# Other urgencies for the mixers' steps in a two-layer hybrid trunk: one list of ranks and six of its offsets

## The chip, the cores and the metric

The kernel runs on one core of one Trainium2 chip. Times are device microseconds (us) of that core. TensorE does the matrix products, VectorE and ScalarE the elementwise work and the moves out of PSUM, GpSimd small tables, and SyncE issues nearly all DMAs. Where the profile says PE, PEld, DVE, ACT, POOL and SP it means TensorE's products, TensorE's weight loads, VectorE, ScalarE, GpSimd and SyncE.

## The reference

Two layers over 256 positions of 1024 channels. Each layer normalises its input, makes one wide projection, runs three mixers on parts of it, gates and sums their outputs, projects, and ends in a squared-ReLU MLP:

```python
def hybrid_layer(x, pos, ...):
    h = rms_norm(x, g_mix)
    z = h @ w_in
    c_q, c_kv, k_rope, u2, q_nsa, kv_nsa, gate_nsa, gate_mix = jnp.split(z, SPLIT_IDX, axis=-1)
    o_a = mla_mixer(c_q, c_kv, k_rope, ...)          # latent attention, 8 heads
    o_b = conv_mixer(u2, ...)                        # gated 31-tap causal convolution
    o_c = nsa_mixer(q_nsa, kv_nsa, gate_nsa, ...)    # attention over compressed, selected and windowed keys
    g_a, g_b, g_c = jnp.split(jax.nn.sigmoid(gate_mix...), N_MIXERS, axis=-1)
    x = x + (g_a * o_a + g_b * o_b + g_c * o_c) @ w_out
    h = rms_norm(x, g_ffn)
    x = x + jnp.square(jax.nn.relu(h @ w_ff1)) @ w_ff2
    return x
```

In both attentions a block of 128 queries makes scores, a softmax over them, and then the **value products**, probabilities times values:

```python
s = jnp.einsum('bqhd,bkhd->bhqk', qb, k) * scale
p = masked_softmax(s, mask)
o = jnp.einsum('bhqk,bkhd->bqhd', p, v)              # 64 value channels a head
```

## The kernel before, in words

**Precision.** The large products split both operands into a high and a low part in a fast single-pass 32-bit format and sum three products (`gemm_a`, L176, and `gemm_b`, L168). The weights arrive as 512 KB pieces by SyncE; ScalarE makes the high part (L162) and VectorE the low one (L163). The attention's value products, the transposes and a few others stay in plain float32, where one product of the program is two TensorE instructions.

**A layer's stages.** First the norm and the projections whose output has positions on partitions (`psA`). Then the mixers with the rest of the wide projection (`psB`, 24 instructions a 128-column tile) and the output projections of each mixer (`wo`). Then the product with `w_out`, then the MLP (`ff`, `f`).

**Steps and urgencies.** The mixers' stage is cut into 58 steps, traced in the order of the list `TRACE`. A step is for instance ("qk", 1), the norm, rotation and transposes of one half's queries and keys; ("gt", m, i), two 128-column tiles of mixer m's gates with their two weight pieces; ("nsa", j) and ("mla", j), half the heads of an attention; ("mq", b) and ("mk", b), the latent attention's queries and keys of one half of the positions; ("tap", i), three or four of the convolution's taps on VectorE; ("cn",), the convolution's norm; ("wo", m, c), a quarter of mixer m's output projection; ("csc",), the scores against the compressed keys; ("lr", n) and ("lrn",), the low-rank inputs and their norms. Each step gets the number 1000 times its place in the list `URGENCY`, and each instruction of the step carries that number:

```python
for name, *args in TRACE:
    tc.cur_priority = base + 1000 * PRIO[(name, *args)]
    steps[name](*args)
```

A planner then writes out the order of each engine's instructions when the program is built: of those that its own cost table takes to be ready, and whose buffer is free, the one with the smallest number goes first. On the chip that order is fixed, and an engine waits at its next instruction until that one can run.

**Late parts.** Some steps raise or lower the number inside, by the table `OFF`: the transposes of `qk` by `qk0` and `qk1` (L433), the compression by `ckv` and `cmp` (L470, L482), the end of `csc` (L549), the transposes of the probabilities by `nT` and `mT` (L583), the heads' transposes by `hT` (L704), and the value products by `nO` (L613) and `mO` (L641).

**The value products.** `nsa_attention` (L594) has three blocks for each j: both pairs of heads for the first 128 queries, then each pair for the last 128. A block makes scores (`nS`, L606), two softmax units (L562), whose probabilities are transposed (`nT`, L586) and copied to SBUF by ScalarE (`nPT`, L588), and the value products `nO` (L621):

```python
for g in range(2):
    gs = slice(64 * g, 64 * g + 64)
    c = j * T + b * P
    mm(po[gs, c:c + P], lhsT=vsw[:, kb, z, gs], rhs=PTs[g][:, u * P:(u + 1) * P], ...)
```

A value product has 64 weight columns and writes 64 of PSUM's partitions, so TensorE's array is tiled by 64 columns for it, and by 128 for its neighbours; the two products of g = 0 and g = 1 lie in the two halves of the array. There are 24 of them for each j, which is 48 TensorE instructions. They end with two products with the compressed keys' probabilities (L625, 128 columns), after which `po`, a PSUM bank of which there is one, is split into `oh` and `ol` and free for the next. `mla_attention` (L629) does the same with three blocks of 8 instructions for each j (`mO`, L649). The compression has products of 32 weight columns (`cmp`, L486 and L498) and one of 32 rows (L512). The probabilities and their transposes live in the tile `pa`, of which there are 6.

Of the kernel before, what the change touches and what calls it, by code (L numbers as in the profile page):

```python
# [53 lines left out]
for _n, _w in _CST:  # L54
# [20 lines left out]
URGENCY = [("csc",), ("mq", 1), ("a1",), ("a",), ("qk", 1), ("lr", 0), ("lr", 1), ("qk", 0), ("mq", 0), ("mk", 0),  # L75
           ("ckv",), ("a2",), ("gt", 1, 2), ("mk", 1), ("glu", 3), ("a0",), ("lr", 2), ("tap", 2), ("gt", 2, 2),
           ("glu", 0), ("glu", 1), ("mla", 1), ("glu", 2), ("mla", 0), ("nsa", 1), ("gt", 2, 0), ("tap", 0),
# [4 lines left out]
PRIO = {s: i for i, s in enumerate(URGENCY)}  # L82

OFF = {"qk0": 11500, "qk1": 6000, "ckv": -10500, "cmp": 14500, "csc": 14500, "nT": 5000, "mT": 12500,
       "nO": 19000, "mO": -8000, "hT": -5500}


@with_exitstack
def trunk_kernel(ctx: ExitStack, tc: tile.TileContext, A, out, depth=DEPTH):
# [8 lines left out]
    def psum(tag, name):  # L98
        return pp.tile([P, 512], F32, tag=tag, name=name, bufs={"mm": 2, "at": 2, "pt": 2, "po": 1, "ch": 1}[tag])
# [149 lines left out]
    def rope(X, n, half, ct, st, name, eng=None):  # L249

        eng = eng or nc.vector
        p = X.shape[0]
        r = 2 * half
        a = sp.tile([P, n, r], F32, tag="ra%d" % (n * r), name=name + "_ra", bufs=2 if n * r > 64 else 1)[:p]
        c = sp.tile([P, n, r], F32, tag="rb%d" % (n * r), name=name + "_rb", bufs=2 if n * r > 64 else 1)[:p]
        ctb = bc(ct.rearrange("p (o r) -> p o r", o=1), [p, n, r])
        stb = bc(st.rearrange("p (o r) -> p o r", o=1), [p, n, r])
        eng.tensor_tensor(out=a, in0=X[:, :, 0:r], in1=ctb, op=ALU.mult)
        eng.tensor_tensor(out=c[:, :, 0:half], in0=X[:, :, half:r], in1=stb[:, :, 0:half], op=ALU.mult)
        eng.tensor_tensor(out=c[:, :, half:r], in0=X[:, :, 0:half], in1=stb[:, :, half:r], op=ALU.mult)  # L260
        eng.tensor_tensor(out=X[:, :, 0:r], in0=a, in1=c, op=ALU.add)

    def layer(l):
# [162 lines left out]
        def nsa_qk(b):  # L426
# [5 lines left out]
            rope(kd.rearrange("p j o d -> p (j o) d"), 8, RN // 2, tk_n[0][:, b], tk_n[1][:, b], "rkn")  # L432
            tc.cur_priority += OFF[("qk0", "qk1")[b]]  # L433
            bs = slice(b * P, (b + 1) * P)
# [23 lines left out]
        def compress_kv():  # L458
            KD = ap_.tile([P, 4, T], F32, tag="big", name="KD", bufs=BIG)
            for b in range(NB):  # L460
# [7 lines left out]
                else:  # L468
                    act(KD[64:128, :, b * P - 1:(b + 1) * P - 1], ptv[64:128], AF.Copy)
            tc.cur_priority += OFF["ckv"]  # L470
            for xi, (wn, pe, w2) in enumerate((("ck1", "pek", "ck2"), ("cv1", "pev", "cv2"))):
# [8 lines left out]
                for i in range(2):  # L480
                    nc.sync.dma_start(out=w1[:, 8 * i:8 * i + 8].rearrange("p k n -> p (k n)"), in_=A[wn][l, i])
                tc.cur_priority += OFF["cmp"]  # L482

# [41 lines left out]
        def compress_scores():  # L525
# [22 lines left out]
            sgv = sg.rearrange("p b (g j n) -> p b j g n", g=2, n=3)  # L548
            tc.cur_priority += OFF["csc"]  # L549
            for b in range(NB):  # L550
# [11 lines left out]
        def softmax_unit(pS, n, gate, name):  # L562
# [19 lines left out]
            now = tc.cur_priority  # L582
            tc.cur_priority += OFF[name + "T"]  # L583
            pt = psum("pt", name + "T")
# [9 lines left out]
        def nsa_attention(jp, o):  # L594
# [3 lines left out]
            for b, js in ((0, (0, 1)), (1, (0,)), (1, (1,))):  # L598
# [13 lines left out]
                now = tc.cur_priority  # L612
                tc.cur_priority += OFF["nO"]  # L613
                for i, j in enumerate(js):
# [483 lines left out]
```

## Time and profile before

| what | value |
|---|---|
| median of 3 runs | 914.36 us (911.64 to 2772.54) |
| the profiled execution | 915.6 us, of which the span from first to last instruction is 913.8 us |
| TensorE busy | 891.2 us, 98% of the span |
| VectorE, ScalarE busy | 654.0 us, 540.4 us |
| mean granted TensorE clock | 0.996 |

A busy share is taken over the whole span. A layer is some 450 us long; its mixers' stage is the first half of it, the MLP the second. TensorE's instructions overlap, so the time that one really takes of the engine is read from start to start, not from its duration.

### The profile page before, as it was taken

Reading aid. Unit: us, or ns where it says so; the run is one execution under the profiler, and the core shown is the slowest. Engines: PE = TensorE matmul, PEld = TensorE weight load, DVE = VectorE, ACT = ScalarE, POOL = GpSimd, SP = SyncE. Lnnn points to the kernel's source line nnn. Section 1 sums busy time; section 2 is a strip of 40 time slices with the busy share of each in tenths; the row PEclk is TensorE's granted clock in tenths of the full one; section 3 lists DMA queues with packets and bytes.
Section 4 is the critical chain, followed back from the end, with each engine's and each line's share of the span. In section 5 each row is a group of like instructions: output and inputs, shape, how many; then the busy total and the mean of one; then the engine's idle time right before and its main releaser. Section 6 shows DMA issues by size and latency. Waiting matters only on the chain.

```text
span 913.8 us, 16151 instructions
## 1 busy us (share of the span) xinstructions
PE 891.2 (98%) x6222; PEld 799.5 (87%) x6222; DVE 654.0 (72%) x1451; ACT 540.4 (59%) x1001; POOL 27.6 (3%) x81
## 2 busy tenths in 40 slices
PE   5999999999999999999999899999999999999998
PEld 4889998689988999999988898977899899999996
DVE  6499899975786755555586998998659685555552
ACT  5467576798456645444354656769967374554430
POOL 4110010000001000000000000000000000000000
PEclk9999999999999999999999999999999999999999
DMA  9335632453664865554452446134446466666501
GB/s 356 141 105 201 231 105 64 141 184 118 205 207 132 310 188 185 190 195 157 138 176 100 138 134 239 59 133 162 142 159 221 129 247 234 188 192 194 188 1 47
DMA packets 42749, 151.55 MB, mean 166 GB/s; under 512 B 4784, under 2 KB 5200, under 8 KB 42672
## 3 DMA queue, kind: packets, MB, share of 16 engines
q1 hardware_dynamic: 42480, 149.99, 49.2%
q8 instruction: 49, 0.80, 0.4%
q0 software_dynamic: 192, 0.53, 0.2%
q14 instruction: 28, 0.23, 0.1%
HBM read 149.45 MB, written 1.05 MB: 165 GB/s over the span
## 4 chain that ended last, share of the span: by engine, by line
PE 90%; DVE 6%; ACT 2%; issue 1%; DMA 1%; SPq 0%; DVEq 0%; ACTq 0%
PE ff L173 7%; PE ff L174 7%; PE ff L172 7%; PE f L180 6%; PE f L181 6%; PE f L182 6%; PE psB L172 6%; PE psB L174 6%; PE psB L173 6%; PE wo L172 3%; PE wo L173 3%; PE wo L174 2%; PE psA L182 2%; PE psA L180 2%; PE psA L181 2%; PE uq L669 2%
## 5 line engine op out<-in xcount | busy, mean ns | idle before, releaser
L163 DVE TENSOR_TENSOR lo<-raw,hi 128x1024 fp32r<-128x1024 f32 (+1 forms) x266 | 316.8, 1210 | 159.9 <-ACT hi L162 120.4
L162 ACT ACTIVATE hi<-raw 128x1024 fp32r<-128x1024 f32 (+1 forms) x266 | 271.8, 1047 | 224.5 <-PE ff L173 74.1
L172 PE MATMUL psB<-hh,hi 128*128 128x256 f32 x592 | 170.0, 288 | 2.6 <-ACT ug L780 2.5
L174 PE MATMUL psB<-hh,lo 128*128 128x256 f32 x592 | 171.0, 290 | 0.7 <-DVE lo L163 0.6
L173 PE MATMUL psB<-hl,hi 128*128 128x256 f32 x592 | 168.4, 285 | 0.0
L173 PE MATMUL ff<-l,hi 128*128 128x256 f32 x512 | 144.2, 282 | 0.0
L172 PE MATMUL ff<-h,hi 128*128 128x256 f32 x512 | 143.9, 281 | 0.0
L174 PE MATMUL ff<-h,lo 128*128 128x256 f32 x512 | 143.6, 281 | 0.0
L172 PEld LDWEIGHTS psB<-hh,hi 128*128 128x128 f32 x592 | 112.8, 191 | 6.3 <-ACT ug L780 3.0
L174 PEld LDWEIGHTS psB<-hh,lo 128*128 128x128 f32 x592 | 112.6, 191 | 3.2 <-DVE lo L163 1.5
L173 PEld LDWEIGHTS psB<-hl,hi 128*128 128x128 f32 x592 | 112.5, 190 | 1.1 <-issue 0.7
L789 DVE SCALAR_TENSOR_TENSOR ca<-upad,cols,ca 128x256 f32<-128x256 f32 x240 | 102.3, 476 | 0.2
L180 PE MATMUL f<-hi,rh 128*128 128x512 f32 x256 | 100.3, 392 | 0.0
L181 PE MATMUL f<-lo,rh 128*128 128x512 f32 x256 | 100.1, 391 | 0.0
L182 PE MATMUL f<-hi,rl 128*128 128x512 f32 x256 | 100.0, 390 | 0.0
L173 PEld LDWEIGHTS ff<-l,hi 128*128 128x128 f32 x512 | 98.0, 191 | 1.8 <-DVE l L217 0.8
L172 PEld LDWEIGHTS ff<-h,hi 128*128 128x128 f32 x512 | 96.1, 188 | 1.3
L174 PEld LDWEIGHTS ff<-h,lo 128*128 128x128 f32 x512 | 96.1, 188 | 0.0
L182 PEld LDWEIGHTS f<-hi,rl 128*128 128x128 f32 x256 | 48.1, 188 | 10.9 <-DVE rl L929 0.7
L180 PEld LDWEIGHTS f<-hi,rh 128*128 128x128 f32 x256 | 48.1, 188 | 9.2
L181 PEld LDWEIGHTS f<-lo,rh 128*128 128x128 f32 x256 | 48.2, 188 | 9.1
L180 PE MATMUL psA<-hi,hh 128*128 128x512 f32 (+1 forms) x96 | 36.4, 380 | 1.5 <-ACT hh L185 1.5
(283 smaller groups left out, 1438.7 us busy)
## 6 DMA issues: line engine op xcount, KB each, us to landing
raw<-in_ff_dram SPq DMA_DIRECT2D x128, 512.0 KB, 4.3
raw<-in_wB_dram SPq DMA_DIRECT2D x74, 512.0 KB, 4.2
raw<-in_wA_dram SPq DMA_DIRECT2D x16, 512.0 KB, 6.5
raw<-in_w_out_dram SPq DMA_DIRECT2D x16, 512.0 KB, 4.2
raw<-in_wo_nsa_dram SPq DMA_DIRECT2D x8, 512.0 KB, 4.3
raw<-in_wo_mla_dram SPq DMA_DIRECT2D x8, 512.0 KB, 4.2
raw<-in_wconv_dram SPq DMA_DIRECT2D x8, 512.0 KB, 3.6
raw<-in_wA_dram SPq DMA_DIRECT2D x8, 312.0 KB, 5.2
```

The source lines that it names most:

```text
L162: act(hi, r, AF.Copy)
L163: tt(out=lo, in0=r, in1=hi.bitcast(F32), op=ALU.subtract)
L172: mm(ps, lhsT=wh(kw), rhs=ah(ka), start=(first and i == 0), stop=False)
L173: mm(ps, lhsT=wh(kw), rhs=al(ka), start=False, stop=False)
L174: mm(ps, lhsT=wl(kw), rhs=ah(ka), start=False, stop=(last and i == n - 1))
L180: mm(ps, lhsT=ah(ka), rhs=wh(kw), start=(first and i == 0), stop=False)
L181: mm(ps, lhsT=ah(ka), rhs=wl(kw), start=False, stop=False)
L182: mm(ps, lhsT=al(ka), rhs=wh(kw), start=False, stop=(last and i == n - 1))
L669: mm(ps[:, :n], lhsT=cq[:, k, b * P:(b + 1) * P], rhs=w[i][:, c0:c0 + n], start=(i == 0), stop=(i == len(ks) - 1))
L789: stt(out=ca[:, i], in0=upad[:, i, k:k + T], scalar=K("wdw", 31 * i + k), in1=ca[:, i], op0=ALU.mult, op1=ALU.add)
```

## The change

The list `URGENCY` is put in another order and six entries of `OFF` get other values. No instruction, tile or buffer is added or taken away; `TRACE` stays. The changed order brings TensorE's array from one tiling to another 64 times in the whole program, where it was 92 times.

```diff
-URGENCY = [("csc",), ("mq", 1), ("a1",), ("a",), ("qk", 1), ("lr", 0), ("lr", 1), ("qk", 0), ("mq", 0), ("mk", 0),
-           ("ckv",), ("a2",), ("gt", 1, 2), ("mk", 1), ("glu", 3), ("a0",), ("lr", 2), ("tap", 2), ("gt", 2, 2),
-           ("glu", 0), ("glu", 1), ("mla", 1), ("glu", 2), ("mla", 0), ("nsa", 1), ("gt", 2, 0), ("tap", 0),
-           ("nsa", 0), ("tap", 1), ("gt", 2, 1), ("lrn",), ("gt", 0, 0), ("wo", 0, 0), ("gt", 2, 3), ("gt", 1, 0),
-           ("wo", 2, 0), ("tap", 7), ("tap", 4), ("gt", 0, 3), ("gt", 0, 1), ("tap", 6), ("tap", 3), ("cn",),
-           ("wo", 0, 1), ("gt", 1, 1), ("gt", 0, 2), ("wo", 0, 2), ("gt", 1, 3), ("wo", 2, 1), ("tap", 5),
-           ("wo", 0, 3), ("wo", 2, 2), ("wo", 2, 3), ("wo", 1, 0), ("wo", 1, 1), ("wo", 1, 2), ("rk",), ("wo", 1, 3)]
+URGENCY = [("mq", 1), ("a",), ("csc",), ("qk", 1), ("gt", 1, 3), ("a1",), ("lr", 0), ("lr", 1), ("qk", 0), ("mq", 0),
+           ("a0",), ("ckv",), ("a2",), ("glu", 3), ("gt", 1, 2), ("tap", 2), ("lr", 2), ("mk", 1), ("glu", 0),
+           ("mla", 0), ("glu", 1), ("mla", 1), ("mk", 0), ("glu", 2), ("gt", 2, 2), ("nsa", 1), ("gt", 2, 0),
+           ("tap", 0), ("nsa", 0), ("wo", 0, 0), ("tap", 1), ("gt", 2, 1), ("lrn",), ("gt", 0, 0), ("tap", 7),
+           ("gt", 2, 3), ("gt", 1, 0), ("gt", 0, 3), ("wo", 2, 0), ("gt", 1, 1), ("gt", 0, 1), ("tap", 4), ("cn",),
+           ("tap", 6), ("tap", 3), ("wo", 2, 1), ("wo", 0, 1), ("wo", 2, 2), ("gt", 0, 2), ("wo", 0, 2), ("tap", 5),
+           ("wo", 0, 3), ("wo", 2, 3), ("wo", 1, 0), ("wo", 1, 1), ("wo", 1, 2), ("rk",), ("wo", 1, 3)]
...
-OFF = {"qk0": 11500, "qk1": 6000, "ckv": -10500, "cmp": 14500, "csc": 14500, "nT": 5000, "mT": 12500,
-       "nO": 19000, "mO": -8000, "hT": -5500}
+OFF = {"qk0": 11500, "qk1": 11000, "ckv": -10500, "cmp": 15000, "csc": 6000, "nT": 4000, "mT": 14500,
+       "nO": 19000, "mO": -6000, "hT": -5500}
```

## Rows read from the trace of the kernel before

**Rows 1.** The page's busy times: us, share of the span, instructions.

```profile
PE 891.2 (98%) x6222; PEld 799.5 (87%) x6222; DVE 654.0 (72%) x1451; ACT 540.4 (59%) x1001; POOL 27.6 (3%) x81
```

**Rows 2.** Busy time by stretch, mixers' stage of layer 1: stretch, its length, engines, clock, DMA.

```profile
46.20:75.40 29.20, 26.22 (x217) 24.90 (x215) 27.90 (x65) 18.66 (x30) 2.70 (x10) 1.00 0.44 142
106.50:140.80 34.30, 34.07 (x320) 31.48 (x318) 32.83 (x121) 25.21 (x66) 2.29 (x2) 1.00 0.39 138
140.80:171.00 30.20, 30.05 (x216) 23.58 (x215) 28.93 (x105) 20.71 (x63) 0.00 (x0) 1.00 0.35 113
171.00:199.30 28.30, 28.21 (x175) 21.22 (x176) 24.96 (x115) 25.02 (x56) 1.05 (x4) 1.00 0.52 174
199.30:227.00 27.70, 27.69 (x243) 25.70 (x241) 15.58 (x41) 25.70 (x63) 0.20 (x1) 1.00 0.35 114
```

**Rows 3.** TensorE in order of time, 172.6 to 175.5 us: start, time, what.

```profile
174.52 0.28 PE L172 MATMUL psB<-hh,hi 128*128 128x256 f32 x1
174.64 0.28 PE L173 MATMUL psB<-hl,hi 128*128 128x256 f32 x1
174.84 0.43 PE L621 MATMUL nO<-nPT,vsw 128*64 128x128 f32 x2
175.21 0.39 PE L174 MATMUL psB<-hh,lo 128*128 128x256 f32 x1
175.43 0.28 PE L172 MATMUL psB<-hh,hi 128*128 128x256 f32 x1
```

**Rows 4.** TensorE in order of time, 207.9 to 209.7 us.

```profile
208.36 0.28 PE L172 MATMUL psB<-hh,hi 128*128 128x256 f32 x1
208.57 0.66 PE L649 MATMUL mO<-mPT,Vm 128*64 128x128 f32 x8
209.16 0.92 PE L638 MATMUL mS<-kTm,qTm 96*128 96x256 f32 x3
```

**Rows 5.** TensorE in order of time, 140.4 to 147.3 us.

```profile
140.83 1.52 PE L621 MATMUL nO<-nPT,vsw 128*64 128x128 f32 x22
...
142.71 0.44 PE L621 MATMUL nO<-nPT,vsw 128*64 128x128 f32 x4
143.08 0.66 PE L586 MATMUL nT<-cst,nP 128*128 128x128 f32 x4
143.67 1.85 PE L621 MATMUL nO<-nPT,vsw 128*64 128x128 f32 x22
```

**Rows 6.** Busy time of L621 alone in stretches around its groups, second j of layer 1.

```profile
156.90:157.90 1.00, 0.87 (x10) 0.63 (x10) 1.00 0.00 0
160.30:161.00 0.70, 0.65 (x6) 0.41 (x6) 1.00 0.00 0
169.80:171.00 1.20, 1.09 (x14) 0.85 (x14) 1.00 0.89 273
...
197.90:198.40 0.50, 0.43 (x2) 0.19 (x2) 1.00 0.76 311
```

**Rows 7.** The program's value products of the first attention by line: count, busy us, mean ns, idle.

```profile
L621 PE MATMUL nO<-nPT,vsw 128*64 128x128 f32 x192 | 17.9, 285 | 0.2
```

**Rows 8.** Who TensorE waited for in 46 to 76 us: us, times, longest.

```profile
PE psB L172 <- ACT ug L780: 1.3, 1, 1.3
PE qS_p L438 <- DVE qn L261: 1.0, 1, 1.0
```

**Rows 9.** TensorE in order of time, 95.6 to 102.2 us.

```profile
96.04 2.29 PE L680 MATMUL css<-ones,csq 128*128 128x1 f32 x20
```

**Rows 10.** Busy time by stretch, columns as in group 2.

```profile
98.30:101.70 3.40, 3.40 (x19) 3.40 (x18) 3.17 (x9) 0.00 (x0) 0.00 (x0) 0.50 0.86 283
...
140.40:143.80 3.40, 3.40 (x39) 2.62 (x39) 3.40 (x13) 2.44 (x7) 0.00 (x0) 1.00 0.00 0
143.80:147.20 3.40, 3.30 (x31) 2.69 (x31) 3.40 (x11) 2.22 (x10) 0.00 (x0) 1.00 0.03 5
```

**Rows 11.** The page's DMA issues: count, KB each, us to landing.

```profile
raw<-in_wB_dram SPq DMA_DIRECT2D x74, 512.0 KB, 4.2
```

## The prediction, made before the change was run

> **What bounds the kernel now.** I read the busy times first. TensorE works 891 of 913.8 us [rows 1], so the kernel ends when TensorE's queue ends, and a change of order helps only as far as it takes time out of that queue: less work in it, or fewer waits. The next view is busy time by stretch, for the mixers' stage, the only one whose order changes. From 106 us on TensorE has no idle time worth a name (0.23 us in 34.3, 0.15 in 30.2, 0.09 in 28.3, 0.01 in 27.7), and only from 46 to 75 us it waits, 3.0 us in 29.2 [rows 2]. VectorE is almost as full there: 27.9 of 29.2, 32.8 of 34.3 and 28.9 of 30.2 us, and has room only later, 3.3 us in 171 to 199 and 12.1 us in 199 to 227 [rows 2]. The third view is TensorE in order of time around the groups of 64-column products, since a busy engine hides the cost of changing its tiling: it must be read from start to start.
>
> **What a change of tiling costs.** A product of the wide projection starts 0.12 us after the one before it (174.52 to 174.64). The first value product behind one starts after 0.20 us (174.64 to 174.84) [rows 3], or 0.21 (208.36 to 208.57) [rows 4]: 0.08 to 0.09 us more. Inside a group, 4 instructions take 0.37 us to the start of the next group (142.71 to 143.08) [rows 5], and 8 take 0.59 (208.57 to 209.16) [rows 4]. So four more cost 0.22, or 0.055 each; 8 would cost 0.44, and the other 0.15 us is the group's own loss, at its start and its end. The first product behind the group keeps its successor back as well: 0.22 us (175.21 to 175.43) instead of 0.12 [rows 3], 0.10 more. Together 0.09 + 0.15 + 0.10 = 0.34 us for a group, which is two changes: 0.17 us each.
>
> By the Trainium skill this could be cheaper. "TensorEngine Tiling (Array Packing)", section Key Properties, says that a new tiling mode drains the engine, and "TensorE: Matmul & The Clock Gate", section "Step-by-step: what each phase is for", puts the array's draining at some 128 cycles: an estimate of 0.053 us at 2.4 GHz, and 28 x 0.053 = 1.5 us in all. The trace disagrees, with 0.17 us a change; I go by the trace.
>
> **What the change removes.** From 92 to 64 is 28 changes, 14 groups, 7 in each layer. The first j's value products already stand in three groups, of 22, 4 and 22 instructions [rows 5]. The second j's 48 are scattered from 156.9 to 198.4 us in nine groups, of 10, 6, 14, 2, 2, 4, 4, 4 and 2 (the first three and the last are in [rows 6]); layer 2 has as many again (192 in all) [rows 7]. Seven groups fewer a layer is just what is left over when these nine become two, so that is where I place them. 14 x 0.34 = **4.8 us** less work in TensorE's queue, all of it where that queue has no idle time.
>
> A second, smaller term: a group of 2 instructions takes 0.37 us (174.84 to 175.21) [rows 3], as long as one of 4. A lone product leaves the other half of the array empty, and costs 0.11 us that a pair would share. The groups of 10, 6, 14, 2, 2 and 2 are of odd numbers of products, so six stand alone in a layer. If they meet their partners, three times 0.11 us go in each layer: **0.7 us**. Bounds for both terms: no partner met, and only the inside and the exit paid (0.25 us a group), 3.5 us; every group as dear as the lone ones (0.08 + 0.26 + 0.10 = 0.44), 6.2 us. I take 4.8 + 0.7 = 5.5.
>
> **What the change moves, and what I cost at nothing.** ("gt", 1, 3) goes from place 47 to 4, but writes a tile that ("gt", 1, 0) allocates, at 36: it comes right behind that and no earlier. Two 512 KB loads and their splits on ScalarE and VectorE come forward with it in SyncE's queue; such a load lands 4.2 us after its issue [rows 11], and the DMA engines are 0.33 to 0.55 busy in this stage [rows 2], so they have room. The other gates, ("wo", 2, 1) and ("wo", 2, 2) change places by a few, each with its loads; the number of bytes and of splits is the same. Cover for all of this is the queue of ready gates and output projections, which filled TensorE to 27.69 of 27.70 us even while the second attention ran [rows 2]; if it fails, TensorE waits by the microsecond, which is the slower rival below. The taps go back a few places ("tap", 4, 6 and 3, from 37, 40 and 41 to 41, 43 and 44), which frees VectorE earlier and puts the convolution's norm later; its output projections are last in the list anyway, and VectorE has 12.1 us free from 199 to 227 us. ("mk", 0) goes from 9 to 22, behind ("mk", 1), and the two halves of the second attention change places: their first scores may come some microseconds later, with the same cover. GpSimd has 27.6 us of work in all and its steps keep their places [rows 1].
>
> **The early waits.** The late part of ("qk", 1) goes from number 10000 to 14000, behind ("glu", 3) at 13000. Its transposes kept TensorE waiting 1.0 us for VectorE's rotation, and the gated unit's PSUM tile, which ScalarE had not emptied, another 1.3 us; these are the longest [rows 8]. At best all 3.0 us of waiting go, 6.0 us in two layers; at worst as many come in addition. VectorE's 27.9 us of work there are unchanged and fill 29.2 us, so a wait that goes at one place is likely to return at another: I take nothing, and keep part of both ends.
>
> **TensorE's clock.** After twenty one-column products from 96.0 us on [rows 9] the granted clock is 0.50, that is 1.2 of 2.4 GHz, for 3.4 us [rows 10], a loss of 1.7 us, once a layer. Step ("lrn",), whose products these are, keeps its neighbours (30 to 32, still behind ("gt", 2, 1)), so I expect it again. At best it goes (3.4 us in all), at worst as much comes in addition.
>
> **The sum.** The profiled execution took 915.6 us, 1.2 above the median of 914.36. 915.6 - 5.5 = 910.1, and with the 1.2 taken off for the median **909 us**, a gain of 0.6%. A measurement of this kernel tells about 2% from no change.
>
> **The rivals.**
>
> *VectorE takes the gain.* By the Trainium skill, "Perfetto Trace Analysis", section "Identifying the Most-Contended Engine", TensorE is to be judged by its weight loads' busy time, and the engine with the highest share is the one to relieve. As a mechanism of this kernel: from 140.8 to 171 us the weight loads fill 23.6 of 30.2 us and VectorE 28.9 [rows 2]. If VectorE were the bound, shorter work on TensorE would become waiting for the low parts of the weights. VectorE's idle time from 140.8 to 199.3 us is 1.3 + 3.3 = 4.6 us; the gain of 2.7 us a layer would fit, but only if its work moved with it. Against: TensorE shows no wait in that stretch, and the taps can go to VectorE's free 12 us. If all is taken, the time stays at 914. Chance 0.2, the remnants included of a count that falls with a cheaper kind of group than I priced.
>
> *The waits from 46 to 75 us go too.* With half to all of the 6.0 us: 903 to 906. For it: another product now stands ahead of the late transposes. Against: VectorE is full. Chance 0.13.
>
> *Slower: TensorE waits for the gathered value products.* They can stand together only when the last transposed probabilities of the group are in SBUF. Until then the finished ones keep their places in the six `pa` tiles, the next softmax units have nowhere to write, and the one bank `po` stays taken, which the second attention needs. TensorE's queue is in order: if ScalarE's last copy is later than the planner thought, every gate and projection behind it waits. A wait of this kind is taken at 1.3 us, the longest seen [rows 8]. Two more a layer, 5.2 us, eat the gain; from there on it is slower. Three give 909 + 7.8 = 917. Against: in the first j 22, 4 and 22 instructions stand within 5 us without a wait [rows 5], at the full clock too [rows 10]. Chance 0.15. A fall of the clock behind the gathered stretch, 1.7 us a layer, would add to it; alone it gives 912, inside my forecast.
>
> **How the numbers follow.** Forecast, 906 to 912, chance 0.52; no gain, 912 to 916, 0.2; waits gone, 903 to 906, 0.13; slower, 916 to 920, 0.15. The range of 903 to 917 leaves out most of the slower case and a little below. Both bounds of 2% (896 and 933) need something that no row shows: 0.02 faster, 0.95 within, 0.03 slower.
>
> **What would show it.** Right: in each layer the 48 instructions of the second j stand in two or three groups, some 16 groups of 32 and 64 columns in all instead of 23; a group still costs some 0.34 us; TensorE's busy time from 106 us to the end of the stage is the same share of a stage that is some 2.7 us shorter; the clock falls once a layer, as before. Wrong: new waits of TensorE for `nPT`, for the low parts, or for PSUM in the wide projection, of over 2.7 us a layer; a different count of groups; or a second fall of the clock.

## The result, and the profile after

The changed kernel takes 908.18 us (median of 9 runs, 906.9 to 910.47) against 913.27 us for the kernel before in the same job: a ratio of 0.9947 [0.9937, 0.9957], a gain of 5.1 us or 0.5%. By the 2% that the prediction set itself this is no change; by the interval it is a small gain. The forecast was 909.0. The profiled execution took 909.84 us, its span 908.1.

The busy times of the changed kernel answer to [rows 1]:

```profile
PE 884.2 (97%) x6222; PEld 797.4 (88%) x6222; DVE 652.6 (72%) x1451; ACT 541.2 (60%) x1001; POOL 29.8 (3%) x81
```

TensorE has the same 6222 instructions and is busy 7.0 us less. Now the stretches of [rows 2] (columns: stretch, its length, TensorE, its weight loads, VectorE, ScalarE, GpSimd, clock, DMA), and behind them two of 3.4 us right after the one-column products, for [rows 10]:

```profile
46.60:76.00 29.40, 26.36 (x221) 25.25 (x220) 28.10 (x65) 19.28 (x31) 2.93 (x10) 1.00 0.45 144
139.00:171.00 32.00, 31.75 (x223) 24.72 (x223) 31.01 (x117) 22.94 (x69) 0.00 (x0) 1.00 0.39 130
171.00:199.00 28.00, 27.91 (x193) 23.44 (x192) 21.96 (x100) 25.02 (x56) 1.05 (x4) 1.00 0.49 168
199.00:227.00 28.00, 28.00 (x247) 26.23 (x246) 16.30 (x42) 23.04 (x55) 0.00 (x0) 1.00 0.35 113
...
98.30:101.70 3.40, 3.27 (x29) 3.07 (x28) 3.17 (x9) 1.24 (x3) 0.00 (x0) 1.00 0.84 264
541.80:545.20 3.40, 3.40 (x18) 3.40 (x17) 3.19 (x10) 0.12 (x1) 0.00 (x0) 0.50 0.87 287
```

The early stretch still waits 3.0 us, and from 139 us on TensorE has 0.3 us of idle time in 88. VectorE, 31.0 of 32.0 us busy from 139 to 171, kept TensorE waiting nowhere there. The clock fell in layer 2 and not in layer 1, where the same products stand in the same places.

TensorE in order of time (start, time, what) answers to [rows 3, 4, 5]:

```profile
139.04 2.18 PE L621 MATMUL nO<-nPT,vsw 128*64 128x128 f32 x34
...
142.50 1.09 PE L621 MATMUL nO<-nPT,vsw 128*64 128x128 f32 x14 [0.22 <-ACT nPT L588]
...
155.87 2.20 PE L669 MATMUL uq<-raw,cq 128*128 128x384 f32 x6
...
172.72 0.28 PE L173 MATMUL psB<-hl,hi 128*128 128x256 f32 x1
172.93 0.43 PE L621 MATMUL nO<-nPT,vsw 128*64 128x128 f32 x2
173.29 0.39 PE L174 MATMUL psB<-hh,lo 128*128 128x256 f32 x1
173.51 0.28 PE L172 MATMUL psB<-hh,hi 128*128 128x256 f32 x1
...
219.64 1.53 PE L649 MATMUL mO<-mPT,Vm 128*64 128x128 f32 x24
221.10 0.66 PE L586 MATMUL mT<-cst,mP 128*128 128x128 f32 x4
...
222.96 1.09 PE L649 MATMUL mO<-mPT,Vm 128*64 128x128 f32 x16
...
227.22 0.66 PE L649 MATMUL mO<-mPT,Vm 128*64 128x128 f32 x8
...
256.79 0.40 PE L180 MATMUL wo<-hi,mh 128*128 128x512 f32 x1
```

The first j stands in two groups, of 34 and 14, where it had three. The second attention's six groups of 8 have become three, of 24, 16 and 8. The price of a group reads as before: 172.72 to 172.93 on the way in, 0.22 us on the way out; and the group of 24 takes 1.46 us from start to start, which is 24 x 0.055 = 1.32 and 0.14 besides. One larger group costs what a small one costs. For the second j, the busy time of L621 alone around its groups, for [rows 6]:

```profile
155.00:156.20 1.20, 0.87 (x10) 0.63 (x10) 1.00 0.00 0
158.30:159.20 0.90, 0.65 (x6) 0.41 (x6) 1.00 0.00 0
167.80:169.20 1.40, 1.09 (x14) 0.85 (x14) 1.00 0.65 240
171.20:171.80 0.60, 0.43 (x2) 0.19 (x2) 1.00 0.98 403
172.80:173.30 0.50, 0.37 (x2) 0.19 (x2) 1.00 0.00 0
215.70:217.00 1.30, 1.09 (x14) 0.85 (x14) 1.00 0.37 132
```

Six groups, where there were nine: only the last four have joined, into one of 14. Every one is still of an odd number of products. So the seven groups that a layer lost are one in the first j, three in the second, and three in the second attention. Who TensorE waited for, in the whole program (us, times, longest), for [rows 8]:

```profile
PE psB L172 <- ACT ug L780: 2.4, 2, 1.2
PE qS_p L438 <- DVE qn L261: 1.9, 2, 1.0
...
PE nO L621 <- ACT nPT L588: 0.4, 2, 0.2
...
PE wo L172 <- DVE gt L860: 0.4, 2, 0.2
```

The wait for the gathered value products exists, for the last copied probabilities as the rival had it, and is 0.2 us a layer; it stands before the second group of the first j.

**Where the profile's 5.7 us went** (span 913.8 to 908.1). Taken between marks that both traces have, layer 1 and layer 2: up to the first compression product 1.6 and 1.3 us; from there to the first `uq` product (L669) 0.3 and 0.45; from there to the first product with `w_out` (L180) 0.9 and 1.0; everything else 0.1 in all. Half of it, 2.9 us, lies ahead of the first product that moved on TensorE in its layer, the first `nO`. One fall of the clock less is 1.7 of that. This is one execution against another, so the experiments had to tell what of it belongs to the change.

### The profile page after: what moved, and what is told of

Its sections match the earlier page's. It is cut to its first block, busy times and chain, and to the rows that moved or that the text cites. A ratio compares the mean times of both kernels' runs of the same rounds, so it can differ in the third digit from the quotient of the medians.

```text
span 908.1 us, 16151 instructions
## 1 busy us (share of the span) xinstructions
PE 884.2 (97%) x6222; PEld 797.4 (88%) x6222; DVE 652.6 (72%) x1451; ACT 541.2 (60%) x1001; POOL 29.8 (3%) x81
## 4 chain that ended last, share of the span: by engine, by line
PE 90%; DVE 6%; ACT 1%; issue 1%; DMA 1%; SPq 0%; DVEq 0%
PE ff L173 7%; PE ff L172 7%; PE ff L174 7%; PE f L180 6%; PE f L182 6%; PE f L181 6%; PE psB L172 6%; PE psB L174 6%; PE psB L173 6%; PE wo L172 3%; PE wo L173 2%; PE wo L174 2%; PE psA L182 2%; PE psA L180 2%; PE psA L181 2%; PE uq L669 2%
## 5 line engine op out<-in xcount | busy, mean ns | idle before, releaser
L172 PE MATMUL psB<-hh,hi 128*128 128x256 f32 x592 | 169.5, 288 | 2.5 <-ACT ug L780 2.4
L173 PE MATMUL psB<-hl,hi 128*128 128x256 f32 x592 | 166.5, 283 | 0.0
L172 PE MATMUL ff<-h,hi 128*128 128x256 f32 x512 | 143.9, 281 | 0.0
L172 PEld LDWEIGHTS psB<-hh,hi 128*128 128x128 f32 x592 | 112.1, 190 | 5.6 <-ACT ug L780 2.9
L789 DVE SCALAR_TENSOR_TENSOR ca<-upad,cols,ca 128x256 f32<-128x256 f32 x240 | 102.2, 474 | 0.2
L180 PE MATMUL f<-hi,rh 128*128 128x512 f32 x256 | 100.3, 392 | 0.0
L172 PEld LDWEIGHTS ff<-h,hi 128*128 128x128 f32 x512 | 96.1, 188 | 1.3
L180 PEld LDWEIGHTS f<-hi,rh 128*128 128x128 f32 x256 | 48.1, 188 | 9.2
L180 PE MATMUL psA<-hi,hh 128*128 128x512 f32 (+1 forms) x96 | 36.2, 377 | 1.9 <-ACT hh L185 1.8
```

The lines of the kernel that those rows point to most:

```text
L172: mm(ps, lhsT=wh(kw), rhs=ah(ka), start=(first and i == 0), stop=False)
L173: mm(ps, lhsT=wh(kw), rhs=al(ka), start=False, stop=False)
L180: mm(ps, lhsT=ah(ka), rhs=wh(kw), start=(first and i == 0), stop=False)
L789: stt(out=ca[:, i], in0=upad[:, i, k:k + T], scalar=K("wdw", 31 * i + k), in1=ca[:, i], op0=ALU.mult, op1=ALU.add)
```

## The experiments

Two theories. **Tiling:** the time goes with the number of groups, wherever they stand. **Clock:** the gain is the fall that one profile has and the other has not, or the early stage. The kernel before was run once more under a name of its own, to see what the comparison gives for no change at all. The first four ran together.

**Only the late groups.** One step moves, so that 12 of the 14 groups go; the first j stays in three groups and the list is otherwise that of before.

```diff
-            ("tap", 6), ("tap", 3), ("cn",), ("wo", 0, 1), ("gt", 1, 1), ("gt", 0, 2),
+            ("tap", 6), ("cn",), ("wo", 0, 1), ("gt", 1, 1), ("tap", 3), ("gt", 0, 2),
```

> One move alone in the list of before, ("tap", 3) from place 41 to 44: the late regrouping, 68 changes of tiling; TensorE's order is that of before up to some 190 us of each layer. Theory 1, that the gain is the 28 changes removed at 0.17 us each: 24 fewer give 4.1 us, 909.2 us where before is at 913.3. Theory 2, that in the traces only about 1.0 us a layer comes from this stretch, and the rest of the gain from falls of TensorE's clock that came in one profile and not in the other: 911.3 us.

Measured: 910.11 us (6 runs) against 913.92, 0.9968 [0.9956, 0.998], so 3.8 us less. The stage from `uq` to `w_out` in the kernel before, and then in this one:

```profile
157.78 2.20 PE L669 MATMUL uq<-raw,cq 128*128 128x384 f32 x6
...
259.63 0.39 PE L180 MATMUL wo<-hi,mh 128*128 128x512 f32 x1
```

```profile
155.45 2.20 PE L669 MATMUL uq<-raw,cq 128*128 128x384 f32 x6
...
255.81 0.39 PE L180 MATMUL wo<-hi,mh 128*128 128x512 f32 x1
```

101.85 us have become 100.36, in layer 2 101.94 have become 100.37: 1.5 us a layer for six groups, at the same order of TensorE up to that place; over the runs the mean clock is 0.9975 here and 0.9981 in the kernel before, so the clock did not give it. One step's place, of the 58, carries most of the change.

**Only the first j.** 88 changes, its value products in two groups.

```diff
-            ("gt", 0, 2), ("wo", 0, 2), ("gt", 1, 3), ("wo", 2, 1), ("tap", 5),
+            ("wo", 0, 2), ("gt", 1, 3), ("wo", 2, 1), ("gt", 0, 2), ("tap", 5),
```

> One move alone in the list of before, ("gt", 0, 2) from place 45 to 48: only the first j's value products are regrouped, 17 and 7 instead of 11, 2 and 11 products, 88 changes. Theory 1: 4 fewer at 0.17 us give 0.7 us, 912.6 us. Theory 2: the value products now wait for their last probabilities, 0.2 us a layer, and 913.0 us is left.

Measured: 913.08 us, 0.9992 [0.9984, 1.0001]. Alone it can't be told from nothing.

**Only the tail of the second j.** ("mk", 0) goes from place 9 to 22: 80 changes, the second j's last groups join, the second attention stays in six.

```diff
-            ("mq", 0), ("mk", 0), ("ckv",),
+            ("mq", 0), ("ckv",),
...
-            ("glu", 2), ("mla", 0),
+            ("glu", 2), ("mk", 0), ("mla", 0),
```

> One move alone in the list of before, ("mk", 0) from place 9 to 22: the second j's last value products stand together, those of the second attention stay in six groups, 80 changes. Theory 1: 12 fewer at 0.17 us give 2.0 us, 911.2 us. Theory 2: half of that, 912.3 us.

Measured: 913.82 us, 0.9997 [0.9989, 1.0006]: no gain, with six groups less. Its waits of TensorE have this row:

```profile
PE mT L708 <- DVE xk L767: 0.7, 2, 0.3
```

0.35 us a layer, because the second attention's keys now come late; at the predicted 0.34 us three groups a layer are worth three times as much. The stage from `uq` to `w_out` is as long as before in layer 1 (101.90 us) and 0.4 us shorter in layer 2 (101.58). Against the kernel before in two profiles (102.0 on average) it is 0.25 us a layer shorter, and with the wait added back three groups give 0.6, 0.2 each. Net of the wait that is half a microsecond in the program, below what these runs can tell.

**The kernel before, again.** Nothing changed.

> The kernel before once more, unchanged, for the granted clock of its runs. Theory 1: 913.3 us and the clock has no part in the gain; it is spread over its runs as over those of the changed kernel, 0.997 to 1.000. Theory 2: the clock falls in both layers in most runs of before, 0.996, and in none or one in those of the changed kernel, each fall some 1.7 us.

Measured: 913.07 us against 913.92, 0.999 [0.9981, 1.0]. So 0.8 us can come of nothing, and the clock fell once in this profile, not twice.

**Both moves.** ("tap", 3) to 44 and ("gt", 0, 2) to 48, with the offsets of before: 64 changes, in the same groups as the changed kernel, by two moves.

```diff
-            ("tap", 6), ("tap", 3), ("cn",), ("wo", 0, 1), ("gt", 1, 1), ("gt", 0, 2), ("wo", 0, 2), ("gt", 1, 3), ("wo", 2, 1), ("tap", 5),
+            ("tap", 6), ("cn",), ("wo", 0, 1), ("gt", 1, 1), ("tap", 3), ("wo", 0, 2), ("gt", 1, 3), ("wo", 2, 1), ("gt", 0, 2), ("tap", 5),
```

> The list of before with the two moves together, ("tap", 3) to 44 and ("gt", 0, 2) to 48, and the offsets of before: 64 changes in the same groups as the changed kernel, from two of the 58 steps. Theory 1, the groups are all of the change: the changed kernel's time, 909, which is also before less 2.9 and 0.9 of the two moves alone. Theory 3, the other moves and the offsets bring something of their own (the early order of VectorE and ScalarE): 911, as the late move alone.

Measured: 908.32 us (5 runs) against 913.58, 0.994 [0.9928, 0.9952]. This is the whole effect of the change. Two further combinations were only planned, not run: with the new offsets and the old list the planner's order of TensorE is that of before, with its 92 changes, and with the new list and the old offsets it is the changed kernel's. So the offsets are not needed for TensorE's order, and of the 58 places two are.

**The changed kernel, again**, in the same job.

> The changed kernel once more, for its clock and the pace of its products in another execution. Theory 1: 908 to 909, the clock spread as in the runs of before. Rival: the gain comes from a faster pace (0.114 and not 0.118 us a product) that its first profile had by chance in layer 2: the stretch from the first wide product to the compression is then as long as in before, and the time nearer to 910.

Measured: 908.38 us, 0.9944 [0.9932, 0.9956]. Three stretches of 3.4 us after the one-column products, of this run and then of the one before it:

```profile
97.30:100.70 3.40, 3.40 (x19) 3.40 (x18) 2.93 (x7) 0.69 (x2) 0.00 (x0) 0.51 0.78 248
```

```profile
97.30:100.70 3.40, 3.40 (x32) 3.40 (x32) 2.83 (x8) 0.62 (x2) 0.00 (x0) 1.00 0.72 230
541.80:545.20 3.40, 3.29 (x29) 3.08 (x29) 3.14 (x9) 1.42 (x3) 0.00 (x0) 1.00 0.86 265
```

The changed kernel had its fall in layer 2 in one run and in layer 1 in the other; the kernel with two moves had none. In this job the mean clock is 0.9981 for the kernel before (11 runs) and 0.9987 for the changed one (6 runs), a difference worth some 0.5 us (an estimate: 0.0006 of 913). The falls come and go in both, and at the same clock the gain is there: over all runs of the two kernels up to this job whose clock is on record, those at 0.998 take 913.9 us before (32 runs) and 909.3 after (6), and those at 1.000 take 912.7 (7) and 907.1 (5). That is 4.7 and 5.6 us, and the clock theory falls.

The rival here, a faster pace of the products in the first profile's layer 2, is settled in part: a second execution keeps the gain, but it had the faster pace there too. How much of the gain may lie in pace is said below, with what stays open.

**The price by itself.** Into the MLP, where nothing else moves, go 60 extra products whose output nobody reads: in each layer two behind every step of the first MLP product but its first step. One kernel has them 64 columns wide (120 changes of tiling more), the other 128 wide (none).

```diff
+                    if gi > 0:
+                        mm(psum("pt", "dm")[0:64, 0:P], lhsT=ident[:, 0:64], rhs=ident, start=True, stop=True)
```

> The kernel before with 60 more products in the MLP, two behind each of its steps but the first, 64 weight columns wide, into a PSUM tile that nothing reads: 120 more changes of tiling where TensorE has neither waits nor other work. Theory 1: 60 times (0.11 of the product and 0.34 of the two changes) give 27 us more, 941. Rival, that a change costs little and the scattered products lost their time otherwise: 60 times 0.11 to 0.16, 921 to 923.

> The same with 128 weight columns: the same 60 products at the same places and no change of tiling. Both theories: 60 times 0.11 to 0.13 us, 920 to 922. The difference to the run with 64 columns is the price of the changes alone.

Measured: 942.05 us with 64 columns (941.74 to 944.59, 4 runs), 923.77 with 128 (921.9 to 926.6, 4 runs). 18.3 us for 120 changes are 0.152 us a change, 0.305 a group; by the spread of the runs the 18.3 is good to some 2 us. TensorE in order of time, 64 columns and then 128:

```profile
302.48 0.28 PE L174 MATMUL ff<-h,lo 128*128 128x256 f32 x1
302.69 0.43 PE L925 MATMUL dm<-cst 128*64 128x128 f32 x2
303.05 0.38 PE L172 MATMUL ff<-h,hi 128*128 128x256 f32 x1
303.27 0.28 PE L173 MATMUL ff<-l,hi 128*128 128x256 f32 x1
```

```profile
304.57 0.28 PE L174 MATMUL ff<-h,lo 128*128 128x256 f32 x1
304.69 0.39 PE L925 MATMUL dm<-cst 128*128 128x128 f32 x2
304.83 0.36 PE L172 MATMUL ff<-h,hi 128*128 128x256 f32 x1
305.03 0.28 PE L173 MATMUL ff<-l,hi 128*128 128x256 f32 x1
```

0.79 us from the first row to the last against 0.46: 0.09 going in, 0.22 inside, 0.02 going out. The 128-wide product keeps its successor back by nearly as much (0.20 instead of 0.12), so most of what the prediction booked as the exit belongs to the change from plain float32 to the fast format. A transpose does the same in the kernel before (the fast product behind `nT` starts at 153.79 us and the next at 153.99). The extra products are lone ones, and in the kernel before a group of an odd number of products takes 0.10 us more than one of an even number; so 0.305 is not quite the price of the groups that the change removed.

**Fewer changes still.** Another list, with 56 changes; its offsets differ from those of before too. Only the new lines are shown.

```diff
+URGENCY = [("mq", 1), ("lr", 0), ("qk", 1), ("a1",), ("a",), ("csc",), ("qk", 0), ("ckv",),
+           ("gt", 1, 3), ("lr", 1), ("glu", 3), ("gt", 1, 2), ("tap", 2), ("mk", 0), ("a0",), ("lr", 2),
+           ("mq", 0), ("mk", 1), ("mla", 0), ("a2",), ("glu", 0), ("glu", 1), ("glu", 2), ("mla", 1),
+           ("lrn",), ("gt", 2, 0), ("gt", 2, 2), ("nsa", 1), ("nsa", 0), ("tap", 0), ("tap", 1), ("gt", 2, 1), ("wo", 0, 0),
+           ("tap", 7), ("wo", 2, 0), ("gt", 0, 0), ("gt", 1, 0), ("gt", 0, 3), ("tap", 6), ("cn",), ("gt", 2, 3),
+           ("gt", 0, 1), ("tap", 4), ("tap", 3), ("wo", 2, 1), ("gt", 0, 2), ("gt", 1, 1), ("wo", 0, 1), ("wo", 2, 2),
+           ("wo", 1, 1), ("wo", 0, 3), ("wo", 2, 3), ("wo", 0, 2), ("wo", 1, 0), ("rk",), ("wo", 1, 3), ("wo", 1, 2), ("tap", 5)]
+OFF = {"qk0": 10500, "qk1": 12000, "ckv": -13500, "cmp": 15000, "csc": 10000, "nT": 4000, "mT": 14500,
+       "nO": 19000, "mO": -7000, "hT": -5500}
```

> The changed kernel with its list and offsets altered further, by a search for the fewest changes of tiling alone: 56, with the value products of the first attention in 11, 6, 7, 15, 2 and 7. Theory 1: 8 changes fewer at the 0.15 us of the run with 64-column products give 1.2 us, 907.1 where the changed kernel has 908.3. Rival, that the count alone decides nothing and new waits take as much as changes give, as after the move of ("mk", 0): 909 to 912.

Measured: 911.86 us (12 runs) against 914.05, 0.9979 [0.997, 0.9989]. Eight changes fewer than the changed kernel, and 3.7 us slower (another job; 3.2 by the two ratios). Its waits, and behind them the one-column products in order of time:

```profile
PE wo L172 <- ACT ob L858: 2.9, 2, 1.5
...
PE mT L708 <- DVE xk L767: 1.1, 2, 0.6
```

```profile
88.13 1.39 PE L680 MATMUL css<-ones,csq 128*128 128x1 f32 x12
...
91.93 0.72 PE L680 MATMUL css<-ones,csq 128*128 128x1 f32 x6
```

The output projections wait for the convolution's output. I took the place of ("tap", 5), the last of its list, for the reason.

The clock differs as well. The twenty one-column products, back to back in [rows 9], stand in three groups of 12, 2 and 6 here, and all 12 runs have a mean clock of 1.000, where the kernel before has 0.9969 in this job (17 runs). A fall of 3.4 us at 0.50 costs 1.7 us and lowers the mean by 0.0019, so 0.0031 is some 2.8 us (an estimate), more than the 2.2 us that this kernel gained.

**The same with ("tap", 5) at place 50.**

```diff
-            ("wo", 1, 1), ("wo", 0, 3), ("wo", 2, 3), ("wo", 0, 2), ("wo", 1, 0), ("rk",), ("wo", 1, 3), ("wo", 1, 2), ("tap", 5)]
+            ("wo", 1, 1), ("tap", 5), ("wo", 0, 3), ("wo", 2, 3), ("wo", 0, 2), ("wo", 1, 0), ("rk",), ("wo", 1, 3), ("wo", 1, 2)]
```

> The list of the kernel with 56 changes, with ("tap", 5) at place 50 instead of 57, so that the convolution's last taps and its norm are not late: 60 changes of tiling. Theory 1 (0.15 us a change, and the 2.9 us that TensorE waited for the convolution's output at L172 are what the kernel with 56 changes lost): 911.9 - 2.9 + 4 x 0.15 = 909.6 us, and no wait for ob; the wait of mT for xk (1.1 us in all) stays, since ("mk", 0) keeps its place. So it is not below the changed kernel's 908.3 although it has 4 changes fewer. Rival (the altered order costs something else that the waits don't show, such as other weights' loads): 911 us or more with the wait for ob gone. Second rival (the count alone decides): 907.5 us.

Measured: 911.77 us (9 runs) against 914.15, 0.9978 [0.9967, 0.9988], with 60 changes. The wait did not go, and that of `mT` for `xk` is 1.0:

```profile
PE wo L172 <- ACT ob L858: 2.9, 2, 1.5
```

So that reason was wrong, and which step of this list makes the convolution late stays open. The sum: 32 changes fewer at 0.152 are 4.9 us, the new waits take back 3.9, which leaves 1.0. The one-column products stand in groups of 12, 2 and 6 again, and the mean clock is 0.9994 against 0.9968 for the kernel before in this job, which by the same estimate gives 2.4 more: 3.4, where 2.4 were measured. At the price in place that is worked out below, 0.24 us a group, it is 3.8 - 3.9 + 2.4 = 2.3. That the count alone decides is refuted.

**One-column products widened**, with a list of 60 changes. Each of the twenty `css` products now makes 64 equal columns, of which one is read.

```diff
+URGENCY = [("mq", 1), ("a",), ("csc",), ("a1",), ("gt", 1, 3), ("lr", 0), ("lr", 1), ("a0",),
+           ("qk", 1), ("qk", 0), ("a2",), ("ckv",), ("glu", 3), ("gt", 1, 2), ("tap", 2), ("mk", 1),
+           ("mq", 0), ("lr", 2), ("glu", 0), ("glu", 1), ("gt", 2, 2), ("mla", 1), ("mla", 0), ("mk", 0),
+           ("glu", 2), ("gt", 2, 0), ("nsa", 0), ("tap", 1), ("wo", 0, 0), ("tap", 0), ("nsa", 1), ("gt", 2, 1), ("tap", 4),
+           ("gt", 0, 0), ("lrn",), ("tap", 7), ("gt", 2, 3), ("gt", 1, 0), ("wo", 2, 0), ("gt", 0, 1), ("gt", 0, 3),
+           ("gt", 1, 1), ("cn",), ("tap", 6), ("tap", 3), ("wo", 2, 1), ("wo", 0, 1), ("wo", 0, 2), ("gt", 0, 2),
+           ("wo", 2, 2), ("tap", 5), ("wo", 1, 0), ("wo", 0, 3), ("wo", 1, 1), ("rk",), ("wo", 1, 2), ("wo", 2, 3), ("wo", 1, 3)]
+OFF = {"qk0": 11500, "qk1": 11000, "ckv": -10500, "cmp": 15000, "csc": 5000, "nT": 4000, "mT": 14500,
+       "nO": 19000, "mO": -6000, "hT": -5500}
...
-    mm(pss[:, o + b:o + b + 1], lhsT=sqs[i][:, b * P:(b + 1) * P], rhs=ones[:, 0:1],
+    mm(pss[:, (o + b) * 64:(o + b + 1) * 64], lhsT=sqs[i][:, b * P:(b + 1) * P], rhs=ones[:, 0:64],
...
```

> The changed kernel with the products of the low-rank norm 64 columns wide instead of one (the same sums, of which one column is read), and the list altered to 60 changes, since the planner's order moves with the width. Theory on the clock: the fall behind these products does not come, the clock is 1.000 in all runs, and the 0 to 1.7 us that it costs are gone from all of them: with 4 changes fewer 906.9. Rival: the fall comes from elsewhere and stays, 907.7 or more.

Measured: 928.66 us (4 runs), 1.0164 [1.0148, 1.018]. Its waits, and the clock of two stretches:

```profile
PE uv L669 <- ACT gt L834: 4.0, 2, 2.0
PE qS_p L438 <- DVE kS L450: 3.4, 2, 1.8
PE cmp L486 <- ACT gt L834: 2.6, 1, 2.6
PE KD_p L464 <- ACT KD L467: 2.6, 2, 1.3
PE cmp L486 <- DVE G L477: 2.2, 1, 2.2
PE nO L621 <- ACT nPT L588: 2.0, 2, 1.0
```

```profile
109.80:113.20 3.40, 3.40 (x33) 2.64 (x26) 2.90 (x9) 0.00 (x0) 0.00 (x0) 0.50 0.71 245
184.80:188.20 3.40, 3.40 (x10) 1.71 (x9) 1.67 (x10) 1.07 (x2) 0.00 (x0) 0.51 0.94 299
```

These six rows are 16.8 us, more than the 14.6 lost; the list had most likely paid for its 60 changes with them, which no run separates. `nO` waits 1.0 us for its transposed probabilities in each layer: this is the slower rival, in another list. The clock fell in four stretches, none of them right behind the `css` products of its layer: in layer 1 TensorE had just waited 1.3 us for `KD` and 2.2 for `G` before the first, and 1.0 for `nPT` and 2.0 for `gt` before the second. The mean clock is 0.992 in all four runs. So what widening does for the `css` products can't be read from this run.

**No version beats the changed kernel** beyond doubt; the one with two moves is its equal.

## Why the prediction was right, and where it was not

- **The bound.** Right. TensorE's queue sets the end, and less of it is less time: TensorE's busy time is 7.0 us less in the two profiles [rows 1], 1.7 of it by the clock, and VectorE, nearly as full, took nothing back.
- **The price.** 0.34 us a group was read from start to start; the extra products give 0.305 (18.3 us / 60). 14 x 0.305 = 4.3 us, where the term was 4.8. In its place it is less: eight layers of four profiles with the late groups gathered take 100.6 us from `uq` to `w_out` on average (100.3 to 101.0), four of the kernel before 102.0 (101.85 to 102.3), 0.23 to 0.24 us for each of six groups. From the first compression product to `uq`, eight layers with the first j in two groups take 50.8 us and twelve with three take 51.1, the wait of 0.2 included. In all that is 2 x (1.4 + 0.3) = 3.4 us. The term that is most likely too large is the exit. Most of its 0.10 us is paid where TensorE goes from plain float32 to the fast format, and the traces have 140 such places in the kernel before and 140 in the changed one: where a group went, a transpose or a score that had stood beside it remained. Without the exit the reading gives 0.09 + 0.15 = 0.24. This is argued and not tested: the kernel with the late groups alone has 146 such places, and its stages are no longer. The estimate from the Trainium skill ("TensorE: Matmul & The Clock Gate", section "Step-by-step: what each phase is for"), 1.5 us in all, is a third of what the extra products measure.
- **The place.** This step failed: "Seven groups fewer a layer is just what is left over when these nine become two, so that is where I place them." Seven do go, but one in the first j, three in the second, and three in the second attention, which I had not counted among the candidates, though six groups of 8 stood there [rows 4]. Since groups of 4 and 8 lose the same 0.15 us inside, and the gathered one of 24 only 0.14, the sum hardly noticed.
- **The lone products.** 0.7 us that did not come. All six groups are still of odd numbers, so their lone products are still alone. Gathering by rank joins neighbours in time; it doesn't pair the two halves.
- **What I costed at nothing.** The early waits are what they were: 2.4 and 1.9 us in two layers, against 1.3 and 1.0 in one [rows 8]. The moved gates, loads and taps cost nothing that a wait shows, apart from 0.4 us for `gt`.
- **The clock.** "I expect it again" was right for the kernel and wrong for the run. With the twenty one-column products back to back the fall comes in some executions and not in others, so it belongs in the range, once up and once down, and not in the sum. With groups of 12, 2 and 6 it came behind them in neither profile, and the mean clock stayed at 0.999 to 1.000 in 21 runs; no run moves these products alone.
- **The rivals.** VectorE did not take the gain. The early waits stayed. The slower one is real: 0.2 us a layer in the changed kernel, 1.0 in the last list above, which lost 14.6 us by this and other waits. That the prediction gave 5.5 us and 5.1 were measured is in part luck: 3.4 to 4.3 of price, where 4.8 was booked and 0.7 for lone products that did not meet, and up to 0.8 that comes of nothing.

What stays open: of the changed kernel's 5.1 us, 0.8 is not accounted for by the price of the extra products, and 1.7 not by the stages in which groups went. The kernel before gains 0.8 against itself. Some 0.7 lies where TensorE's order is the same: from layer 1's first product with `w_out` to layer 2's first compression product, four profiles with the first j in two groups take 291.4 to 292.2 us and four with three groups 292.3 to 292.7, each fall of the clock taken off at 1.7. The pace of the products differs there (last section). Whether that belongs to the change is not shown.

## What to carry to other kernels

When an order is searched by one number, such as changes of tiling, price the number by itself first (the same extra product with and without the change), and then read the waits of each candidate: here 64 changes beat 56 and 60, for a late producer (2.9 us) costs as much as 19 changes. Read the granted clock of each candidate's runs too: by the estimate above it is worth as much as the list of 56 gained in all. Look for the few moves that carry a large re-ranking; two of 58 places did all of it. Run the old kernel against itself before explaining a part of one per cent.

## What the runs showed of the hardware that was not expected

The pace of the fast products differs between executions of one program, at the full clock. The products of L172 alone, in the same stretch of the changed kernel, in its first run and then in its second:

```profile
76.00:92.00 16.00, 12.74 (x46) 8.45 (x46) 1.00 0.54 166
```

```profile
76.00:92.00 16.00, 12.99 (x48) 8.84 (x48) 1.00 0.53 163
```

48 of them instead of 46 in 16 us, at the same DMA share (0.54 and 0.53). From start to start a fast product of this stretch takes 0.118 us in the first run and 0.113 in the second (medians). In layer 2 the first profile of the changed kernel has 48 in 16 us (from 522 us) where the kernel before has 46 (from 525 us). That is most of the 1.3 us by which the two profiles differ there ahead of the first moved product. I found nothing in the traces that it follows, and its cause is open.
